# A dilated convolution on one core: warm-up matmuls taken out, the first load split in two, the last two stores split into four

## The chip, the cores and the metric

The kernel runs on one core of a Trainium2 chip. The metric is the device time of an execution, in microseconds (us). Each kernel of a comparison is run several times, in rounds that alternate it with the kernel before on the same chip. The profile is one execution, traced; its span is about 1.8 us shorter than the time of that execution.

In the text and in the views, PE is the matrix engine (TensorE) and PEld its weight loads; DVE is VectorE, ACT ScalarE, POOL or Pool GpSimd, SP SyncE. PEclk, the granted clock, is the share of PE's full clock that it was given. DMA means the transfers between HBM and SBUF. A semaphore is a counter on which an engine waits until others have raised it. Dummy matmuls are matmuls whose results nobody uses.

## The reference

```python
# x: [16, 64, 64, 64] float32, weight: [128, 64, 3, 3] float32, dilation 2
x_pad = np.pad(x, ((0, 0), (0, 0), (2, 2), (2, 2)))
for b, co, ci, kh, kw in all_of_them:
    output[b, co] += weight[co, ci, kh, kw] * x_pad[b, ci, kh*2:kh*2+h, kw*2:kw*2+w]
```

The output is [16, 128, 64, 64] float32. So 17.07 MB must be read from HBM and 33.55 MB written, whatever the arithmetic looks like. Stores are two thirds of the traffic.

## The kernel before

Two images of 64 channels fill the 128 partitions: an image pair. There are eight pairs, 0 to 7, and a pair is computed in four groups of 16 rows. A group needs 30 matmuls into three PSUM tiles; ScalarE copies one of them to SBUF, and VectorE adds it to each of the other two, into the output tile `osb`. The parts that matter here, shortened:

```python
XB = 4                                    # four float32 image pairs fit in SBUF
x32pool = tc.tile_pool(name="x32pool", bufs=XB)
opool   = tc.tile_pool(name="opool", bufs=3)      # three output tiles, 4 MB each

def load(pb, rows):                       # rows: where to cut, [H] is one transfer
    ...
    for hi in rows:
        nc.sync.dma_start(out=t[:, lo * W : hi * W], in_=x_pair[pb, :, lo * W : hi * W])

def store(pb, m, lo, hi):                 # Pool issues, but SP for the last pair
    queue = nc.gpsimd if pb < npairs - 1 else nc.sync
    queue.dma_start(out=out_img[2 * pb + m, :, lo * W : hi * W], in_=o_tiles[pb][...])

nc.sync.dma_start(out=w32, in_=weight...)         # weights first
for pb in range(min(XB, npairs)):
    load(pb, [H])
...
run_warm(14)                              # 14 dummy matmuls of 512 columns on zeros
# ... weights cast, transposed on PE, copied to w_sb ...
run_warm(14)                              # 14 more, until the first image is there
...
for G in range(ngroups):                  # 32 groups
    ...                                   # 30 matmuls, p_sb copy, two adds, casts ahead
    if ahead[0] >= NG * (freed[0] + 1) and freed[0] + XB < npairs:
        load(freed[0] + XB, [H])          # when all of an old pair is cast
    if pb in (0, npairs - 1) and g % 2 == 1:      # first and last pair: in halves
        for m in range(2):
            store(pb, m, (g - 1) * GR, (g + 1) * GR)
    elif 0 < pb < npairs - 1 and g == NG - 1:     # others: whole images
        for m in range(2):
            store(pb, m, 0, H)
```

A whole image is stored in rows of 16 KB per partition, half an image in rows of 8 KB, a quarter in rows of 4 KB. They show up in the trace as packets of those sizes.

Of the kernel before, what the change touches and what calls it, by code (L numbers as in the profile page):

```python
# [10 lines left out]
def kernel(  # L11
# [18 lines left out]
    nc = tc.nc  # L30

    B, CI, H, W = x.shape
# [5 lines left out]
    d = 2  # L38

    P = 128  # L40
    f32 = mybir.dt.float32
    f16 = mybir.dt.float16
# [4 lines left out]
    GR = 16  # L47
    NG = H // GR
    NBLK = GR // 4
    NH = GR // 2 * W  # L50
    npairs = B // 2
# [5 lines left out]
    wpool = ctx.enter_context(tc.tile_pool(name="wpool", bufs=1))  # L57
# [4 lines left out]
    ppool = ctx.enter_context(tc.tile_pool(name="ppool", bufs=1, space=bass.MemoryType.PSUM))  # L62
# [10 lines left out]
    def load(pb, rows):  # L73

        t = x32pool.tile([P, HW], f32, tag="x32", name="x32")
        x32_tiles[pb] = t
        lo = 0
        for hi in rows:
            nc.sync.dma_start(out=t[:, lo * W : hi * W], in_=x_pair[pb, :, lo * W : hi * W])
            lo = hi  # L80
# [19 lines left out]
    def store(pb, m, lo, hi):  # L100
        queue = nc.gpsimd if pb < npairs - 1 else nc.sync
        queue.dma_start(  # L102
            out=out_img[2 * pb + m, :, lo * W : hi * W],
            in_=o_tiles[pb][:, m * HW + lo * W : m * HW + hi * W],
        )
# [4 lines left out]
    w32 = wpool.tile([CO, CI * KH * KW], f32, name="w32")  # L110
    nc.sync.dma_start(out=w32, in_=weight.rearrange("o i h w -> o (i h w)"))  # L111
    for pb in range(min(XB, npairs)):
        load(pb, [H])

    ident = wpool.tile([P, P], f16, name="ident")
    make_identity(nc, ident)


    warm = wpool.tile([P, 512], f16, name="warm")
    nc.vector.memset(warm, 0.0)  # L120
    wp = ppool.tile([P, 1024], f32, tag="p", name="wp")

    def run_warm(n):
        for _ in range(n):
            nc.tensor.matmul(out=wp[:, 0:512], lhsT=warm[:, 0:P], rhs=warm)  # L125

    run_warm(14)


    KINDS = 5  # L130
# [13 lines left out]
    for q, n in ((0, 8), (8, 7)):  # L144
        wt = apool.tile([P, 1024], f32, tag="ab", name="wt")
        for t in range(q, q + n):
            nc.tensor.matmul(
                out=wt[:, (t - q) * CO : (t - q + 1) * CO],
                lhsT=wd[:, t * 2 * CI : (t + 1) * 2 * CI],
                rhs=ident,  # L150
# [5 lines left out]
    def product(ps, src, kind, blk0, nblk, first, last):  # L156

        for j in (1, 0, 2):
            dw = (j - 1) * d
            o0, o1 = max(0, -dw), W - max(0, dw)  # L160
            t = kind * KW + j
            for hb in range(2):
                pp = slice(hb * CI, (hb + 1) * CI)
                rhs = src(pp, dw + o0, dw + o1)
                po = ps[:, hb * NH + blk0 * 2 * W : hb * NH + (blk0 + nblk) * 2 * W]
                po = po.rearrange("p (r w) -> p r w", w=W)[:, :, o0:o1]
                nc.tensor.matmul(  # L167
                    out=po,
                    lhsT=w_sb[pp, t * CO : (t + 1) * CO],
                    rhs=rhs,  # L170
                    start=first and j == 1,
                    stop=last and j == 2,
                )

    def blocks(x16, b0, n, e):

        v = x16.rearrange("p (b e r w) -> p b e r w", e=2, r=2, w=W)
        return lambda pp, c0, c1: v[pp, b0 : b0 + n, e, :, c0:c1]

    run_warm(14)  # L180
    ahead = [0, 0]

    def prepare(casts, sums):

        while ahead[0] < min(casts, ngroups):
            cast(ahead[0])
            ahead[0] += 1
        while ahead[1] < min(sums, ngroups):
            rowsum(ahead[1])
            ahead[1] += 1  # L190
# [5 lines left out]
    for G in range(ngroups):  # L196
        pb, g = divmod(G, NG)
        x16 = x16_tiles[pb]
        xs = xs_tiles[pb].rearrange("p (r w) -> p r w", w=W)
        if g == 0:  # L200
            o_tiles[pb] = opool.tile([P, 2 * HW], f32, tag="osb", name="osb")
        o = o_tiles[pb].rearrange("p (m b e q) -> p m b e q", m=2, e=2, q=2 * W)
        b0 = g * NBLK

        psP = ppool.tile([P, 2 * NH], f32, tag="p", name="psP")
        sv = lambda pp, c0, c1: xs[pp, g * GR // 2 : (g + 1) * GR // 2, c0:c1]
        product(psP, sv, 0, 0, NBLK, True, True)

        psA = apool.tile([P, 2 * NH], f32, tag="ab", name="psA")
        product(psA, blocks(x16, b0, NBLK, 1), 1, 0, NBLK, True, False)  # L210
        z = 1 if g == 0 else 0
        product(psA, blocks(x16, b0 + z - 1, NBLK - z, 1), 2, z, NBLK - z, False, True)

        psB = apool.tile([P, 2 * NH], f32, tag="ab", name="psB")
        product(psB, blocks(x16, b0, NBLK, 0), 3, 0, NBLK, True, False)
        z = 1 if g == NG - 1 else 0
        product(psB, blocks(x16, b0 + 1, NBLK - z, 0), 4, 0, NBLK - z, False, True)

        p_sb = spool.tile([P, 2 * NH], f32, tag="psb", name="p_sb")
        nc.scalar.copy(out=p_sb, in_=psP)  # L220
        pv = p_sb.rearrange("p (m b q) -> p m b q", m=2, q=2 * W)

        def evac(e, ps):
            nc.vector.tensor_tensor(  # L224
                out=o[:, :, b0 : b0 + NBLK, e],
                in0=ps.rearrange("p (m b q) -> p m b q", m=2, q=2 * W),
                in1=pv,
                op=add,
            )

        evac(0, psA)
        prepare(min(G + 3 + (G + 1) // 2, G + 1 + LOOK), G + 3)
        evac(1, psB)

        if ahead[0] >= NG * (freed[0] + 1) and freed[0] + XB < npairs:
            load(freed[0] + XB, [H])
            freed[0] += 1
        if pb in (0, npairs - 1) and g % 2 == 1:
            for m in range(2):
                store(pb, m, (g - 1) * GR, (g + 1) * GR)  # L240
        elif 0 < pb < npairs - 1 and g == NG - 1:
            for m in range(2):
                store(pb, m, 0, H)
# [35 lines left out]
```

## Time and profile before

| | before |
|---|---|
| time, median of 3 (lowest to highest) | 127.46 us (127.44 to 127.64) |
| span of the profiled execution | 125.6 us |
| moved by DMA | 50.78 MB, mean 404 GB/s |
| last VectorE add ends | 111.9 us |
| last data packet ends | 124.0 us |
| last store's semaphore full | 124.5 us |

From the profile page of the kernel before: busy time by engine, then rows of the span in 40 slices of 3.14 us, each digit a busy share in tenths; GB/s is what DMA moved in each slice.

```profile
PE 108.3 (86%) x1003; PEld 53.8 (43%) x1003; DVE 89.9 (72%) x105; ACT 66.9 (53%) x71; POOL 9.3 (7%) x22
...
PE   6998999999999999999979999999999999920000
...
DMA  5999999999999999999999999999999999999970
GB/s 160 383 444 418 438 423 402 381 415 444 391 457 418 410 418 436 441 444 418 423 423 425 428 449 423 428 418 423 428 449 423 428 428 418 412 431 407 428 331 16
```

Two rows are full of nines, PE and DMA, and the reader must find out which of them the time follows. PE stops at slice 36; DMA goes on for three slices after it.

The chain of work that ended last, kernel before, in order of time (start us, length us, what), with the stretch from 67.2 to 108.1 us, all PE, left out:

```profile
37.37 0.52 POOL out_dram L102
37.89 26.48 DMA out_dram<-osb
64.37 0.03 issue
...
64.49 1.24 DVE osb L224
65.73 0.04 issue
65.77 1.44 PE psB L167 x12
...
108.13 1.28 PE psA L167 x12
```

VectorE waited until 64.4 us for a store of pair 1 to leave an output tile free, and PE waited for VectorE. After that PE runs back to back to its end.

The start of the kernel before, from the timeline (start us, busy us, engine, line, operation, out<-in, shapes, count, and the idle time just before with what ended it):

```profile
1.19 5.08 PE L125 MATMUL wp<-warm 128*128 128x512 f16 x14 [1.19 <-DVE warm L120]
...
6.11 1.00 PE L147 MATMUL wt<-ident,wd 128*128 128x128 f16 x15
...
6.95 3.19 PE L125 MATMUL wp<-warm 128*128 128x512 f16 x14
...
8.80 2.10 ACT L88 CAST x_157<-x_80 128x1152 f16<-128x1152 f32 x2 [0.25 <-DMA x_80<-in_x_dram]
...
10.47 0.81 PE L167 MATMUL psP<-xs,w_sb 64*128 64x512 f16 x6 [0.34 <-DVE xs L98]
```

The dummies fill PE from 1.2 us until the first image pair is loaded and cast. The granted clock becomes full at 5.05 us.

The table by stretch, kernel before (stretch in us, its length, busy time and count of PE, weight loads, VectorE, ScalarE and Pool, granted clock, DMA share, GB/s). A DMA share of 1.00 means that all 16 DMA engines had a packet in progress.

```profile
core 0: us, PE busy (x) PEld busy (x) DVE busy (x) ACT busy (x) POOL busy (x), PEclk, DMA share, GB/s
...
20.00:25.00 5.00, 5.00 (x52) 2.43 (x50) 4.35 (x7) 4.06 (x5) 0.00 (x0) 1.00 1.02 388
25.00:32.00 7.00, 7.00 (x69) 3.21 (x66) 6.04 (x7) 4.71 (x5) 1.05 (x2) 1.00 0.99 414
...
99.00:107.00 8.00, 8.00 (x80) 4.37 (x78) 6.88 (x8) 2.89 (x3) 1.06 (x2) 1.00 1.00 422
107.00:120.00 13.00, 3.51 (x36) 1.70 (x31) 4.11 (x4) 1.01 (x1) 0.00 (x0) 0.78 1.00 420
```

### The profile page before, as it was taken

Reading aid. Unit: us, or ns where it says so; the run is one execution under the profiler, and the core shown is the slowest. Engines: PE = TensorE matmul, PEld = TensorE weight load, DVE = VectorE, ACT = ScalarE, POOL = GpSimd, SP = SyncE. Lnnn points to the kernel's source line nnn. Section 1 sums busy time; section 2 is a strip of 40 time slices with the busy share of each in tenths; the row PEclk is TensorE's granted clock in tenths of the full one; section 3 lists DMA queues with packets and bytes.
Section 4 is the critical chain, followed back from the end, with each engine's and each line's share of the span. In section 5 each row is a group of like instructions: output and inputs, shape, how many; then the busy total and the mean of one; then the engine's idle time right before and its main releaser. Section 6 shows DMA issues by size and latency. Waiting matters only on the chain.

```text
span 125.6 us, 2342 instructions
## 1 busy us (share of the span) xinstructions
PE 108.3 (86%) x1003; PEld 53.8 (43%) x1003; DVE 89.9 (72%) x105; ACT 66.9 (53%) x71; POOL 9.3 (7%) x22
## 2 busy tenths in 40 slices
PE   6998999999999999999979999999999999920000
PEld 2453444544454445444435555555555555500000
DVE  0732888988898888988649998889888988760000
ACT  4558686966666666666654666666666433300000
POOL 2000003030002001100210003000200120000000
PEclk9999999999999999999999999999999999997555
DMA  5999999999999999999999999999999999999970
GB/s 160 383 444 418 438 423 402 381 415 444 391 457 418 410 418 436 441 444 418 423 423 425 428 449 423 428 418 423 428 449 423 428 428 418 412 431 407 428 331 16
DMA packets 4186, 50.78 MB, mean 404 GB/s; under 512 B 464, under 2 KB 464, under 8 KB 592
## 3 DMA queue, kind: packets, MB, share of 16 engines
q0 software_dynamic: 2304, 29.36, 55.1%
q1 hardware_dynamic: 1872, 21.27, 40.8%
q8 instruction: 8, 0.13, 0.4%
q14 instruction: 2, 0.02, 0.0%
HBM read 17.07 MB, written 33.55 MB: 403 GB/s over the span
## 4 chain that ended last, share of the span: by engine, by line
PE 54%; DMA 27%; DVE 4%; DVEq 1%; ACT 1%; issue 1%; POOL 0%; SPq 0%
PE psA L167 22%; DMA out_dram<-osb 21%; PE psB L167 21%; PE psP L167 11%; DMA x_80<-in_x_dram 6%; DVE osb L224 4%; ACT x_157 L88 1%; DVEq L274 1%; DVE xs L98 1%; POOL out_dram L102 0%; SPq L111 0%; DVEq L224 0%
## 5 line engine op out<-in xcount | busy, mean ns | idle before, releaser
L167 PEld LDWEIGHTS <-w_sb 64*128 64x128 f16 x960 | 49.9, 94 | 50.6 <-issue 1.0
L220 ACT COPY p_sb<-psP 128x1024 f32<-128x1024 f32 x32 | 32.4, 1012 | 37.7 <-PE psP L167 18.2
L224 DVE TENSOR_TENSOR osb<-psA,p_sb 128x1024 f32<-128x1024 f32 x32 | 39.2, 1224 | 15.2 <-PE psA L167 11.7
L224 DVE TENSOR_TENSOR osb<-psB,p_sb 128x1024 f32<-128x1024 f32 x32 | 39.0, 1218 | 0.0
L167 PE MATMUL psP<-xs,w_sb 64*128 64x496 f16 (+1 forms) x192 | 25.7, 371 | 0.3 <-DVE xs L98 0.3
L102 POOL DMA_DIRECT2D out_dram<-osb x16 | 8.6, 540 | 91.3 <-DVE osb L224 91.3
L125 PE MATMUL wp<-warm 128*128 128x512 f16 x28 | 8.3, 460 | 1.2 <-DVE warm L120 1.2
L167 PE MATMUL psB<-x_695,w_sb 64*128 64x496 f16 (+3 forms) x48 | 5.6, 365 | 0.7 <-DVE osb L224 0.7
L167 PE MATMUL psB<-x_1017,w_sb 64*128 64x496 f16 (+3 forms) x48 | 5.6, 365 | 0.0
L167 PE MATMUL psB<-x_856,w_sb 64*128 64x496 f16 (+3 forms) x48 | 5.6, 365 | 0.0
L167 PE MATMUL psB<-x_1178,w_sb 64*128 64x496 f16 (+3 forms) x48 | 5.6, 365 | 0.0
L167 PE MATMUL psA<-x_1178,w_sb 64*128 64x496 f16 (+3 forms) x48 | 5.6, 365 | 0.0
L167 PE MATMUL psA<-x_1017,w_sb 64*128 64x496 f16 (+3 forms) x48 | 5.6, 365 | 0.0
L167 PE MATMUL psA<-x_856,w_sb 64*128 64x496 f16 (+3 forms) x48 | 5.6, 365 | 0.0
L167 PE MATMUL psA<-x_695,w_sb 64*128 64x496 f16 (+3 forms) x48 | 5.6, 365 | 0.0
L167 PE MATMUL psA<-x_157,w_sb 64*128 64x496 f16 (+3 forms) x48 | 5.6, 365 | 0.0
L167 PE MATMUL psA<-x_240,w_sb 64*128 64x496 f16 (+3 forms) x48 | 5.6, 365 | 0.0
L167 PE MATMUL psA<-x_532,w_sb 64*128 64x496 f16 (+3 forms) x48 | 5.6, 365 | 0.0
L167 PE MATMUL psA<-x_369,w_sb 64*128 64x496 f16 (+3 forms) x48 | 5.6, 365 | 0.0
L167 PE MATMUL psB<-x_240,w_sb 64*128 64x496 f16 (+3 forms) x48 | 5.6, 365 | 0.0
L167 PE MATMUL psB<-x_157,w_sb 64*128 64x496 f16 (+3 forms) x48 | 5.6, 365 | 0.0
L167 PE MATMUL psB<-x_369,w_sb 64*128 64x496 f16 (+3 forms) x48 | 5.6, 365 | 0.0
(35 smaller groups left out, 66.3 us busy)
## 6 DMA issues: line engine op xcount, KB each, us to landing
out_dram<-osb POOLq DMA_DIRECT2D x12, 2048.0 KB, 17.6
out_dram<-osb POOLq DMA_DIRECT2D x4, 1024.0 KB, 20.8
out_dram<-osb SPq DMA_DIRECT2D x4, 1024.0 KB, 11.8
x_80<-in_x_dram SPq DMA_DIRECT2D x1, 2048.0 KB, 7.6
x_82<-in_x_dram SPq DMA_DIRECT2D x1, 2048.0 KB, 12.0
x_84<-in_x_dram SPq DMA_DIRECT2D x1, 2048.0 KB, 17.9
x_86<-in_x_dram SPq DMA_DIRECT2D x1, 2048.0 KB, 23.8
x_245<-in_x_dram SPq DMA_DIRECT2D x1, 2048.0 KB, 17.5
```

The costliest lines, as they stand in the source:

```text
L88: nc.scalar.copy(out=x16_tiles[pb][:, lo * W : hi * W], in_=x32_tiles[pb][:, lo * W : hi * W])
L98: nc.vector.tensor_tensor(out=s, in0=v[:, :, 0], in1=v[:, :, 1], op=add)
L102: queue.dma_start(out=out_img[2 * pb + m, :, lo * W : hi * W], in_=o_tiles[pb][:, m * HW + lo * W : m * HW + hi * W],)
L125: nc.tensor.matmul(out=wp[:, 0:512], lhsT=warm[:, 0:P], rhs=warm)
L167: nc.tensor.matmul(out=po, lhsT=w_sb[pp, t * CO : (t + 1) * CO], rhs=rhs, start=first and j == 1, stop=last and j == 2,)
L220: nc.scalar.copy(out=p_sb, in_=psP)
L224: nc.vector.tensor_tensor(out=o[:, :, b0 : b0 + NBLK, e], in0=ps.rearrange("p (m b q) -> p m b q", m=2, q=2 * W), in1=pv, op=add,)
L274: with _tile.TileContext(nc) as tc:
```

## The change

The intent: drop the dummy matmuls; let the first half of pair 0 arrive early, so that work can start without waiting for all of it; store the last half images in quarters, so that SP issues 16 transfers in place of 13 and the very last one owns the last of the eight semaphores that are waited for at the end.

```diff
     for pb in range(min(XB, npairs)):
-        load(pb, [H])
+        load(pb, [H] if pb else [32 + d, H])
 ...
-    warm = wpool.tile([P, 512], f16, name="warm")
-    nc.vector.memset(warm, 0.0)
-    wp = ppool.tile([P, 1024], f32, tag="p", name="wp")
-
-    def run_warm(n):
-        for _ in range(n):
-            nc.tensor.matmul(out=wp[:, 0:512], lhsT=warm[:, 0:P], rhs=warm)
-
-    run_warm(14)
 ...
-    run_warm(14)
 ...
-        if pb in (0, npairs - 1) and g % 2 == 1:
+        if pb == npairs - 1 and g == NG - 1:
+            for m in range(2):
+                for lo in (2 * GR, 3 * GR):
+                    store(pb, m, lo, lo + GR)
+        elif pb in (0, npairs - 1) and g % 2 == 1:
             for m in range(2):
                 store(pb, m, (g - 1) * GR, (g + 1) * GR)
```

## The prediction

> **What bounds the kernel.** Transfers. The page's DMA row reads 9 tenths in slices 2 to 38 of 40; the table by stage gives a DMA share of 1.00 to 1.01 from 10.5 to 110.7 us at 416 to 429 GB/s. 50.6 MB cross HBM, 118 us at 429 GB/s. PE looks critical as well (the chain of waits gives it 54%, back to back from 65.8 to 109.4 us), but the last VectorE add ends at 111.9 us, while the DMA engines drain queued stores until 124.0 us (their packets). The last store's semaphore fills at 124.5 us; then come 1.1 us of closing waits, of which three pairs after that of the last store take 0.06 us each. So PE has microseconds to spare at the end. The chain also shows VectorE waiting for a store until 64.4 us: DMA set the pace.
>
> **Removed.** 28 dummy matmuls (8.3 us of PE, none on the DMA path). In the trace the matmul spacing falls at 5.0 us from 0.43 us, half of full speed: without the first 14 the transposes and first real groups will run at half clock. The Trainium skill (TensorE: Matmul & The Clock Gate, Part 1) says that full clock comes after about 3.4 us of sustained activity; this trace agrees roughly, 1.2 to 5.0 us. A full-speed group of 30 products takes 3.17 us; I estimate 2 to 4 us of PE work slowed by half, a loss of 1.5 to 3 us. The transposes, which waited for dummies until 5.9 us, can start about 1 us earlier, but at half speed. PE's end: hardly later, at most 3 us, because at the 64 us wait it meets DMA again: all loads are in by then, and the bytes moved fix when that store lands.
>
> **Added.** The first half of image pair 0 lands at about 6 us in place of 8.8. The first cast cannot use all of it: ScalarE copies weights until 8.6 us. The first product comes near 9.9 in place of 10.47. No bytes change. Packets: 8 KB took 309 ns, 16 KB 611 ns, hence about 7 ns per packet beyond its bytes. 2 MB of stores in 4 KB rows in place of 8 KB are 16 more packets per engine, +0.11 us; the split load +0.06 us (estimates).
>
> **Moved.** SP issues 16 transfers, not 13: with eight rotating semaphores the last store gets the last one waited for, saving three waits, 0.19 us, after the end. PE has 56 fewer instructions; the instruction queue moved eight 16 KB packets, the last at 111.5 us after PE's program had ended. It may vanish: up to 0.6 us, only if it sits on the slowest DMA engine.
>
> **Sum, on the critical path:** -0.19 (waits), +0.17 (packets), -0.2 (instruction packet, weighted by chance): about 0.2 to 0.3 us less. Split load and missing dummies should be worth nothing: DMA is saturated from 4 us on. Predicted 127.2 us, range 126.4 to 127.8 (8 in 10). Faster by over 2%: 3%; within 2%: 94%; slower by over 2%: 3%.
>
> **What would show it.** DMA row still 9s to slice 38; last data packets near 123.5 to 124.2 us; the closing wait on the last store followed at once by the drain; first psP product near 10 us, its group taking about 5 us; granted clock full only after 12 to 16 us; last VectorE add between 110 and 114 us.
>
> **What would make it wrong.** A clock that stays at half for long, so that PE ends after about 118 us; DMA queues running empty near 20 us because casts, and with them the release of load buffers, come late; 4 KB rows costing much more than 7 ns a packet; the spread between DMA engines at the end changing by a microsecond.

## The result, and the profile after

| | before | after |
|---|---|---|
| time, median of 6, same chip | 127.45 us (127.29 to 127.72) | 127.38 us (127.24 to 127.64) |
| ratio after to before | | 0.9995, 95% interval 0.9977 to 1.0012 |
| span of the profiled execution | 125.6 us | 125.8 us |
| first product starts | 10.47 us | 9.57 us |
| full granted clock from | 5.05 us | 14.29 us |
| stores of pair 6 issued from | 100.1 us | 100.6 us |
| last VectorE add ends | 111.9 us | 112.4 us |
| last data packet ends | 124.0 us | 124.5 us |

A ratio here is the mean time of one kernel's fast runs over that of the other's in the same rounds, so it is not quite the ratio of the medians in the table. The two kernels take the same time.

From the profile page after, the lines that answer to those of before:

```profile
PE 103.6 (82%) x975; PEld 53.6 (43%) x975; DVE 89.9 (71%) x104; ACT 66.9 (53%) x71; POOL 9.3 (7%) x22
...
PE   0519999999999999999999999999999999920000
...
DMA  4999999999999999999999999999999999999980
GB/s 130 374 439 448 427 427 417 383 414 453 414 411 432 443 414 448 427 419 422 438 432 427 435 417 422 432 437 432 417 427 427 437 391 427 422 393 430 405 327 18
```

PE now rests in the first slices, and the DMA row has not moved. Look at the slice that begins at 100.6 us, the 33rd: 391 GB/s, where before had 428. It is the first hint of what the prediction overlooked.

The start after, from the timeline:

```profile
4.34 0.50 PE L136 MATMUL wt<-ident,wd 128*128 128x128 f16 x3 [4.34 <-DVE wd L124]
...
5.16 1.64 PE L136 MATMUL wt<-ident,wd 128*128 128x128 f16 x12 [0.31 <-DVE wd L127]
...
7.91 2.10 ACT L88 CAST x_127<-x_80 128x1152 f16<-128x1152 f32 x2
...
9.57 1.44 PE L156 MATMUL psP<-xs,w_sb 64*128 64x512 f16 x6 [2.78 <-DVE xs L98]
...
14.90 0.81 PE L156 MATMUL psP<-xs,w_sb 64*128 64x512 f16 x6
```

The first half of the load had landed at 6.8 us, but the cast starts only near 8 us and without idle time ahead of it: ScalarE was copying weights until then. The first product starts 0.9 us earlier than before, as a result of the split load and of transposes that no longer queue behind dummies. The first group then takes 5.3 us (9.57 to 14.90) where a group at full clock takes 3.2: PE reaches the second group at 14.9 us, 1.4 us later than before (13.5). Such starts scatter, though: in the traces of four other kernels here that open exactly as the kernel before, the second group began between 13.7 and 14.6 us, later when the first load landed later.

The table by stretch, after:

```profile
20.00:25.00 5.00, 5.00 (x52) 2.66 (x50) 4.27 (x6) 3.71 (x4) 1.20 (x2) 1.00 1.01 398
25.00:32.00 7.00, 7.00 (x72) 3.62 (x68) 6.35 (x7) 4.69 (x5) 1.05 (x2) 1.00 0.99 422
...
99.00:107.00 8.00, 8.00 (x81) 4.10 (x78) 6.88 (x9) 3.04 (x3) 1.05 (x2) 1.00 0.99 412
107.00:120.00 13.00, 4.02 (x40) 1.92 (x36) 4.62 (x4) 1.01 (x1) 0.00 (x0) 0.74 0.99 413
```

From 99 to 107 us DMA moved 10 GB/s less than before. The page's share of 1.00 and 0.99 hides it; counting packets in half-microsecond steps shows the 16 DMA engines 87% and 78% busy in the two steps from 101.0 us (before 97% and 99%).

One more reading of the trace is needed. A transfer of 128 partitions raises its semaphore 16 times (29 transfers before, 464 arrivals), which is read here as once for each of the 16 DMA engines. The 16 times of the last store show how evenly the engines end:

| last store's 16 arrivals | first | median | 15th | last | from the last to the end of the span |
|---|---|---|---|---|---|
| before | 121.4 | 122.5 | 123.3 | 124.5 us | 1.08 us |
| after | 122.1 | 122.3 | 123.6 | 124.9 us | 0.90 us |

The end is set by one late engine in both kernels. The closing stretch is 0.18 us shorter after, as the intent said; the late engine is 0.45 us later in this one profiled execution, although the median engine is not.

### The profile page after: what moved, and what is told of

Same layout as the page of the kernel before. It is cut to its first block, busy times and chain, and to the rows that moved or that the text cites. A ratio compares the mean times of both kernels' runs of the same rounds, so it can differ in the third digit from the quotient of the medians.

```text
span 125.8 us, 2288 instructions
## 1 busy us (share of the span) xinstructions
PE 103.6 (82%) x975; PEld 53.6 (43%) x975; DVE 89.9 (71%) x104; ACT 66.9 (53%) x71; POOL 9.3 (7%) x22
## 4 chain that ended last, share of the span: by engine, by line
PE 81%; DVE 3%; DMA 2%; ACT 1%; DVEq 1%; issue 0%
PE psA L156 32%; PE psB L156 31%; PE psP L156 17%; DMA w_78<-in_weight_dram 2%; PE wt L136 1%; DVE osb L212 1%; DVEq L266 1%; ACT x_127 L88 1%; DVE wd L127 1%; DVE wd L124 1%; ACT w_sb L143 0%; DVE w_sb L142 0%; DVE xs L98 0%; DVEq L212 0%
## 5 line engine op out<-in xcount | busy, mean ns | idle before, releaser
L156 PEld LDWEIGHTS <-w_sb 64*128 64x128 f16 x960 | 52.3, 95 | 51.8 <-issue 5.1
L156 PE MATMUL psP<-xs,w_sb 64*128 64x496 f16 (+1 forms) x192 | 26.5, 379 | 2.8 <-DVE xs L98 2.8
L156 PE MATMUL psA<-x_127,w_sb 64*128 64x496 f16 (+3 forms) x48 | 6.7, 420 | 0.0
L156 PE MATMUL psB<-x_127,w_sb 64*128 64x496 f16 (+3 forms) x48 | 6.3, 397 | 0.0
L136 PE MATMUL wt<-ident,wd 128*128 128x128 f16 x15 | 2.1, 309 | 4.7 <-DVE wd L124 4.3
L156 PE MATMUL psB<-x_502,w_sb 64*128 64x496 f16 (+3 forms) x48 | 5.6, 365 | 0.0
L156 PE MATMUL psB<-x_210,w_sb 64*128 64x496 f16 (+3 forms) x48 | 5.6, 365 | 0.0
L156 PE MATMUL psB<-x_339,w_sb 64*128 64x496 f16 (+3 forms) x48 | 5.6, 365 | 0.0
L156 PE MATMUL psB<-x_665,w_sb 64*128 64x496 f16 (+3 forms) x48 | 5.6, 365 | 0.0
L156 PE MATMUL psB<-x_826,w_sb 64*128 64x496 f16 (+3 forms) x48 | 5.6, 365 | 0.0
L156 PE MATMUL psB<-x_987,w_sb 64*128 64x496 f16 (+3 forms) x48 | 5.6, 365 | 0.0
L156 PE MATMUL psB<-x_1148,w_sb 64*128 64x496 f16 (+3 forms) x48 | 5.6, 365 | 0.0
L156 PE MATMUL psA<-x_339,w_sb 64*128 64x496 f16 (+3 forms) x48 | 5.6, 365 | 0.0
L156 PE MATMUL psA<-x_502,w_sb 64*128 64x496 f16 (+3 forms) x48 | 5.6, 365 | 0.0
L156 PE MATMUL psA<-x_987,w_sb 64*128 64x496 f16 (+3 forms) x48 | 5.6, 365 | 0.0
L156 PE MATMUL psA<-x_210,w_sb 64*128 64x496 f16 (+3 forms) x48 | 5.6, 365 | 0.0
L156 PE MATMUL psA<-x_665,w_sb 64*128 64x496 f16 (+3 forms) x48 | 5.6, 365 | 0.0
L156 PE MATMUL psA<-x_826,w_sb 64*128 64x496 f16 (+3 forms) x48 | 5.6, 365 | 0.0
## 6 DMA issues: line engine op xcount, KB each, us to landing
x_298<-in_x_dram SPq DMA_DIRECT2D x1, 2048.0 KB, 14.9
```

The lines of the kernel that those rows point to most:

```text
L136: nc.tensor.matmul(out=wt[:, (t - q) * CO : (t - q + 1) * CO], lhsT=wd[:, t * 2 * CI : (t + 1) * 2 * CI], rhs=ident,)
L156: nc.tensor.matmul(out=po, lhsT=w_sb[pp, t * CO : (t + 1) * CO], rhs=rhs, start=first and j == 1, stop=last and j == 2,)
```

## The experiments

Twelve kernels ran, all with correct results, in three calls. "Before" is the kernel before on the same chip in the same rounds: medians 127.50, 127.44 and 127.42 us of 11 runs. The scatter should be kept in mind: single runs of the kernel before went up to 128.26 us.

### The parts of the change, one by one

**No dummies, nothing else.** The kernel before without the definition of `run_warm` and its two calls.

```diff
-    warm = ...; wp = ...; def run_warm(n): ...
-    run_warm(14)
 ...
-    run_warm(14)
```

> The kernel before without its 28 dummy matmuls, nothing else. Theory (DMA engines are saturated, PE has slack): ratio to before 0.998 to 1.002; full clock only near 14 us, as in the changed kernel; last VectorE add 0 to 2 us later than 111.9 us; last data packet still 123.5 to 124.5 us. Rival (PE paces the kernel, and in the changed kernel a loss of about 1.4 us there was paid back by the split load): +0.8 us or more, ratio 1.006 or more.

Measured: 127.70 us, ratio 1.0033, interval 1.0000 to 1.0066. The full clock came at 15.9 us, the last VectorE add ended at 113.8 us, the stores of pair 6 were issued at 102.0 us. The table by stretch has DMA short near 101 us:

```profile
99.00:107.00 8.00, 8.00 (x82) 4.35 (x80) 7.32 (x9) 2.68 (x4) 1.05 (x2) 1.00 0.93 389
```

Neither wording fits well. The time rose by less than the rival asked for, and the interval ends just at 1. One run of six, at 129.11 us, makes up about half of the rise of the mean. But DMA lost 33 GB/s over 8 us, about 0.6 us of its full rate, in a place where the prediction had seen only saturation.

**Split load, nothing else.**

```diff
-        load(pb, [H])
+        load(pb, [H] if pb else [32 + d, H])
```

> The kernel before with only the first load split in two. Theory: PE may start earlier, but the transfers behind it land about 0.15 to 0.2 us later (in the changed kernel the second transfer of 2 MB landed at 13.5 us, before at 13.4), so +0.1 to +0.2 us, ratio 1.000 to 1.002. Rival (an earlier first product is worth something): -0.4 us or more, ratio 0.997 or less.

Measured: 127.52 us, ratio 1.0003, interval 0.9989 to 1.0016: no difference that can be told. The median arrival of the next load was at 13.60 us, before 13.36.

**Quarters, nothing else.** The `if` and `elif` of the change, in the kernel before.

> The kernel before with only the last half images in quarters. SP then issues 15 transfers, so the last store has the last semaphore but one. Theory: two of three closing waits saved (-0.12 us), packets of 4 KB instead of 8 KB +0.1 us: ratio 0.998 to 1.002, and the trace shows about 0.95 us from the last landing to the end in place of 1.1. Rival (smaller last transfers let the end start sooner, or balance the DMA engines): -0.5 us or more, ratio 0.996 or less.

Measured: 127.38 us, ratio 0.9989, interval 0.9977 to 1.0001. From the last arrival to the end 0.95 us, as expected. The rival fails.

**No dummies and the split load, without quarters.** The two edits above together.

> Without dummies and with the split first load, without quarters: the missing cell between the run that only drops the dummies (ratio 1.0033, 95% interval 1.0000 to 1.0066) and the one that only splits the load (1.0003). If the split load pays back what the missing dummies cost (PE 2.8 us behind the kernel before at the second group without it, 1.4 us behind with it), ratio 0.999 to 1.001 and store issues of image pair 6 near 100.6 us. If the load does nothing for it, ratio 1.002 to 1.006, store issues near 102 us.

Measured: 127.78 us, ratio 1.0025, interval 0.9990 to 1.0060: inconclusive in time. The six times fall in two sets, 127.42 to 127.47 and 128.10 to 128.54. In the trace the split load did pay back PE's loss: pair 6 was stored from 100.6 us and not 102.0 (one trace of each kernel, and such starts scatter by about 1 us).

**The whole change with the dummies put back.** `run_warm` and its calls are restored in the changed kernel.

> The changed kernel with its dummies put back. 16 transfers of SP, so the last store has the last semaphore, and PE as early as in the kernel before. If removing the dummies is free in the presence of the split load: ratio 0.998 to 1.001, the same as the changed kernel. If the dummies are still worth something: 0.995 to 0.998.

Measured: 128.06 us, ratio 1.0035, interval 0.9994 to 1.0077; again two sets, 127.45 to 127.69 and 128.43 to 128.82. Neither expectation is met, and this kernel is not shown to improve on either.

The kernel before has such slower runs too (128.05 and 128.26 of its 11). The profiled executions of these two kernels both fell in the slower set, and the arrivals show what sets them apart from the kernel before:

| last store's arrivals | time of that run | median engine | 15th | last engine |
|---|---|---|---|---|
| before | 127.34 us | 122.5 | 123.3 | 124.5 us |
| no dummies, split load | 128.10 us | 122.3 | 123.6 | 125.3 us |
| change with dummies | 128.50 us | 122.5 | 124.2 | 125.8 us |

The median engine ends at the same time; the last engine alone is 0.8 to 1.3 us later. So what these two slower executions lost is, in their traces, the lateness of one DMA engine; no trace of a faster execution of the same kernels was kept to compare. Why it differs from execution to execution stays open.

**The closing waits** can be read from these traces without a stopwatch. SP had issued 13, 14, 15 or 16 transfers in these kernels, and the stretch from the last arrival to the end was 1.08 (before, 13), 1.01 (both kernels with only the load split, 14), 0.95 (quarters, 15) and 0.90 us (16, with and without dummies): 0.06 us for each wait saved, as predicted.

### How late may PE be?

**PE about 4 us late.** In the changed kernel, 34 dummies just before the first real matmuls.

```diff
+    # warm, wp and run_warm as in the kernel before
 ...
+    run_warm(34)
     ahead = [0, 0]
```

> The changed kernel with 34 dummy matmuls just before the first real ones, which should put PE about 4 us behind the changed kernel all the way (last VectorE add near 116 us). Theory 1 (as predicted: PE has 7 us of slack at the end, since the last DMA engine drains until 124 us): +0 to +0.5 us, ratio 1.000 to 1.004. Theory 2 (the slack is small and lies near 101 us, where the stores of image pair 5 run out before those of pair 6 are issued; the changed kernel's faster DMA engines idle there already, and only the late engine's 2 us or so of lag hide it): the DMA row shows a hole near 103 to 106 us and the time rises by 1.2 to 2.5 us, ratio 1.009 to 1.02. Rival (PE paces everything): +4 us, ratio 1.031.

Measured: 130.69 us, ratio 1.0233, interval 1.0196 to 1.0271. The last VectorE add ended at 116.8 us, 4.4 us later than after. From the profile page of this run:

```profile
DMA  5999999898999999999999999999999949999991
GB/s 148 360 446 416 451 431 411 304 315 340 441 424 416 444 424 439 426 426 439 416 426 426 439 416 431 431 431 421 391 416 446 411 198 406 421 424 403 413 407 47
```

and from its table by stretch:

```profile
20.00:25.00 5.00, 5.00 (x50) 2.70 (x48) 4.04 (x5) 4.50 (x5) 0.48 (x1) 1.00 0.89 347
25.00:32.00 7.00, 7.00 (x73) 3.96 (x70) 6.35 (x8) 5.21 (x6) 1.77 (x4) 1.00 0.97 330
...
99.00:107.00 8.00, 8.00 (x83) 4.47 (x79) 7.37 (x9) 3.62 (x5) 1.05 (x2) 1.00 0.81 336
```

Seven microseconds of slack at the end do not exist. DMA loses time at two places. Near 103 to 106 us the stores of pair 5 are nearly done and pair 6 is not (198 GB/s in the 33rd slice); its stores are issued at 105.07 us and their first packets start at 106.17. Counting packets in progress, the engines idled 1.69 us on average from 99 to 107 us (before 0.02): this is a hole. The other place was named in the prediction as what could make it wrong, but not in this run's expectation: near 22 to 32 us. ScalarE, which copies `psP` for every group, casts the image pairs in between, so a late PE makes late casts. The load of pair 4 was issued at 22.1 us (before 16.2, after 17.6), when the four pairs loaded before it were nearly all in and the first store was not yet issued (24.5).

Only part of this early loss is a queue that ran empty: the engines idled 0.65 us on average from 20 to 32 us (before 0.04). From 26 to 30 us they were busy all the time, as the share of 0.97 in the table hints, and still moved only 221 to 384 GB/s, because load packets of 16 KB took 0.75 to 1.10 us on average in place of 0.61. Why they did was not found.

The two losses add up. DMA moved in the three stretches 8,214 KB before (5 x 388 + 7 x 414 + 8 x 422) and 6,733 KB here. The missing 1,481 KB are 3.45 us at 429 GB/s: 1.85 us in the first two stretches, 1.60 us in the last. The measured difference of medians is 3.25 us; the two traced executions differ by 3.63 us. The sum is not exact: from 32 to 99 and from 107 to 120 us another 251 KB, 0.6 us, are missing.

**The same, and every pair stored in halves.**

```diff
-        elif pb in (0, npairs - 1) and g % 2 == 1:
+        elif g % 2 == 1:
```

> The same late PE (34 dummy matmuls), with every image pair stored in halves as soon as a half is done, so that the stores do not run out while a whole pair is computed. Theory 2: the hole near 104 us goes and the time returns to that of the kernel before, ratio 0.998 to 1.004. If the time of the run with the late PE came from anything but stores running out (PE itself, load buffers released late), it stays as slow as that run.

Measured: 130.44 us, ratio 1.0229, interval 1.0201 to 1.0257. The hole near 104 us is gone (every half-microsecond step from 29 to 123 us is over 95% busy), but the time did not return. Taken alone, this would have felled the theory. The next run shows part of the reason.

**Kernel before, every pair stored in halves.**

```diff
-        if pb in (0, npairs - 1) and g % 2 == 1:
+        if g % 2 == 1:
```

> The kernel before with every image pair stored in halves. Theory 2 with its second part (the end is set by the latest DMA engine, which does not idle near 101 us in the kernel before): the idle of the other engines near 101 us (about 0.4 us) goes, but the time stays, ratio 0.998 to 1.002. Rival (that idle is time lost): ratio 0.997 or less.

Measured: 128.25 us, ratio 1.0063, interval 1.0048 to 1.0078. Both wordings miss: halves cost 0.8 us. The trace has 1,536 more data packets, 96 for each engine. A packet of 16 KB took 611 ns and one of 8 KB 309 ns, so two halves take 7 ns more than a whole; 96 times 7 ns is 0.67 us, most of it. So in the run ahead of this one about 0.8 us of packets had been laid over what closing the hole gave back. Even then 3.25 - 1.60 + 0.8 gives +2.45 us, and +3.0 was measured; 0.55 us of that run stays unexplained. (The execution that was traced was the fastest of its four, 2.53 us above the traced one of the kernel before.) The kernel before also had hardly a hole to fill: from 99 to 107 us its engines idled 0.02 us by the count of packets in progress, not the 0.4 us that the expectation names.

**Late PE, pair 6 alone in halves.** This closes the hole near 104 us with a sixth as many extra packets.

```diff
-        elif pb in (0, npairs - 1) and g % 2 == 1:
+        elif pb in (0, npairs - 2, npairs - 1) and g % 2 == 1:
```

> The run with 34 dummies and PE about 4 us late (ratio 1.0233), with image pair 6 alone stored in halves, which costs only 128 more packets of 8 KB per image (estimate +0.1 us). If the hole near 104 us is what cost the time: the hole goes, ratio 1.006 to 1.014. If the cost lies in the first 30 us (load of image pair 4 issued at 22 us, when the loads before it land at 23 us: DMA rate of 158 to 375 GB/s from 22 to 25 us): ratio 1.018 to 1.024. Both places can share it: 1.014 to 1.018.

Measured: 129.72 us, ratio 1.0176, interval 1.0136 to 1.0216. Its table by stretch:

```profile
20.00:25.00 5.00, 5.00 (x52) 2.68 (x48) 4.05 (x5) 4.61 (x5) 0.59 (x1) 1.00 0.91 338
25.00:32.00 7.00, 7.00 (x72) 3.89 (x70) 6.36 (x8) 5.10 (x6) 1.66 (x4) 1.00 0.98 349
...
99.00:107.00 8.00, 8.00 (x82) 4.47 (x80) 7.37 (x9) 3.62 (x5) 1.72 (x4) 1.00 0.98 410
```

The late hole is closed (410 GB/s for 336), the early one is not (338 and 349 for 347 and 330). By the same sum 801 KB are missing, 1.87 us; measured +2.3 us. The traced executions differ by 1.96 us. So both places share the cost of a late PE, by the bytes. In time this is less firm: the ratio fell from 1.0233 to 1.0176 with intervals that overlap, on two chips, and no run closed the early place alone. This is the third of the three expectations, at the edge to the second.

**Kernel before, PE 2 us late.**

```diff
-    run_warm(14)          # the second call
+    run_warm(23)
```

> The kernel before with 9 more dummies before the first real matmuls, at full clock, so that PE starts about 2 us later and nothing else changes. At 64 to 66 us PE has about 0.9 us of waiting for a store to give up, so the stores of image pair 6 should be issued about 1.1 us later than 100.1 us. Theory (little slack there, hidden partly by the lag of the latest engine): idle of the DMA engines near 101 to 103 us of about 1 us, and +0.1 to +0.6 us, ratio 1.001 to 1.005. As predicted at first (7 us of slack): ratio 0.999 to 1.001.

Measured: 127.54 us, ratio 1.0003, interval 0.9978 to 1.0028. Pair 6 was stored from 101.1 us, 1.0 us later than before: the other microsecond was given up at the 64 us wait, as expected. Counting packets in progress, the engines idled 0.4 us on average between 5 and 120 us (before 0.1), and the time did not rise. The late engine would explain how that can be: its share of the last store of pair 5 arrived at 104.7 us, 1.2 us after the next engine's, so it had packets while the others waited for pair 6. An idle moment of fifteen engines would then be free as long as the sixteenth is the one that ends last. The run without dummies agrees: its engines idled 0.8 us on average from 99 to 107 us, and its last store's median arrival came 0.9 us later than before (123.4 for 122.5 us), but the last arrival only 0.2 us later (124.7 for 124.5 us).

### What the late engine is not

**Kernel before, all stores issued by SP.** Theory A is that the late engine and the long packets both come from the transfers that Pool issues.

```diff
-        queue = nc.gpsimd if pb < npairs - 1 else nc.sync
+        queue = nc.sync
```

> The kernel before with all stores issued by SP instead of Pool for all but the last image pair. What is left at the end in both kernels is one DMA engine that finishes about 1.2 us after the next and 2 to 3 us after most, and near 21 to 24 us the packets of loads become longer (up to 1 us in place of 0.61) just as the first stores issued by Pool begin. Theory A[...]: the long packets near 21 us go, the engines finish within 1 us of each other, and the time falls by 1 to 2.5 us (ratio 0.98 to 0.992). Theory B (the late engine is late for another reason, such as the instruction packets): the same 1 us or more of lateness and ratio 0.996 to 1.01. Loads now queue behind stores in one queue; if that starves PE, the time rises by several us.

Measured: 127.82 us, ratio 1.0029, interval 1.0014 to 1.0044. Theory A falls as an explanation of the end: the last store's arrivals spread from 121.2 to 124.9 us. The slow stretch of loads did not go either, it moved (304 GB/s in the slice from 25.2 us, when SP's queue came to the first stores). One part of A seems to survive: in the kernel before, the last engine fell behind the 15th from 0.06 us at 64.4 us to 1.6 us at 109.7 us, while only Pool's stores ran; with SP's stores that gap shrank, from 1.3 to 0.3 us, over the same stretch. But it shrank with Pool's stores as well: in the trace of the next run, which is the kernel before up to its last store, from 1.33 us at 65.6 us to 0.12 us at 99.6 us. So this gap does not tell the two apart. The Trainium skill (DMA: Bandwidth & Descriptors, Latency and other measured facts) says that two of the 16 engines are usually slower, and gives as a best guess the descriptor rings of transfers issued from GpSimd. No run here shows it: the lateness remains without such transfers, and the records name no engine.

**Less work for one engine.** The idea rests on an assumption that no record shows: that the engine numbered highest serves partitions 120 to 127. A last store that leaves them out would take its eight packets of 8 KB from it (2.4 us at 309 ns each).

```diff
+        parts = ((120, 128), (0, 120)) if (pb, m, hi) == (npairs - 1, 1, H) else ((0, P),)
+        for p0, p1 in parts:
             queue.dma_start(out=out_img[2 * pb + m, p0:p1, ...], in_=o_tiles[pb][p0:p1, ...])
```

> The kernel before with the very last store of 1 MB issued as partitions 120 to 127 and then 0 to 119[...]. If the engine that ends 1.2 us after the next one is that one: last landing about 123.3 to 123.7 us in place of 124.5, ratio 0.993 to 0.997. If it is another: last landing 124.5 to 124.9 us, ratio 1.000 to 1.004. In both cases one engine should be done about 2.4 us earlier than it was.

Measured: 127.70 us, ratio 1.0019, interval 1.0005 to 1.0034. The last store has 15 arrivals in place of 16, so one engine was left out, but this tells nothing about the late one: the transfer of 120 partitions itself ran slowly. From 120 to 124 us DMA moved 224 to 333 GB/s, packets of 8 KB took up to 2.2 us, and its arrivals came between 123.0 and 125.2 us. Which engine is late stays open.

## Why the prediction was right

**The time: right.** 127.2 us was predicted and 127.38 measured, in the range, and "within 2%" was right. The predicted gain of 0.2 to 0.3 us is no larger than what the interval leaves open (0.3 us less to 0.15 us more), so the runs confirm that nothing changed, and not the sum of terms.

**DMA bounds the kernel: right.** Bytes, the DMA row and the median engine's end (122.5 and 122.3 us) did not change.

**Missing dummies and split load are worth nothing: right for the whole, for a thinner reason than given.** "DMA is saturated from 4 us on" was read from averages. In truth the DMA queue runs out at two places when PE is late: near 23 us, if the load of pair 4 comes late (0.65 us idle with 34 dummies, and slow packets after it), and near 101 us, where the last stores of pair 5 end just as those of pair 6 are issued (1.69 us idle). The changed kernel is 1.4 us late at the second group, gives 0.9 us back because it no longer has to wait at 64 us (there is no DMA wait there in its chain), and reaches pair 6 half a microsecond late. That is free, as the run with 2 us shows. The prediction had foreseen the wait at 64 us but not looked at the hand-over near 101 us; that the loss fitted in there was luck.

**The step that failed: "So PE has microseconds to spare at the end."** The spare time was measured at the wrong place, at the last store, where 12 us of queued stores hide anything. It has to be measured at each hand-over, where one batch of transfers runs out and the next has to be there. Ending the last add 1.0 us later than the kernel before was free within 0.3%; ending it 4.9 us later cost 3.25 us, although it ended at 116.8 us, before the 118 us that the prediction named as the limit.

**The sum of small terms: the signs right, nearly all unresolved in time.** The waits gave 0.18 us (predicted 0.19), read in the trace. For 16 packets more per engine 0.11 us was estimated; the run with 96 more cost 0.8 us, so a sixth of it, 0.13 us, agrees, and so do the packets themselves (4 KB took 159 ns, two of them 9 ns more than one of 8 KB, 0.14 us for 16). The split load was estimated at 0.06 us; the second load arrived about 0.15 us later (its median arrival was at 13.57 us on average in the seven traces with a split load, at 13.42 us in the seven without), so this term looks too small, although the time of the run with it alone rose by nothing that can be told. The eighth packet of the instruction queue did vanish (7 in place of 8), and the predicted mean gain of 0.2 us from it did not show: the late engine was not earlier. These terms cancel to within the scatter.

**What would show it.** First product "near 10 us" was 9.57, its group 5.3 us for "about 5", full clock 14.29 us within "12 to 16", last add 112.4 us within "110 and 114". The last data packet, at 124.49 us, missed "123.5 to 124.2": the late engine.

**Not settled:** whether dropping the dummies alone costs 0.3%, since that interval ends at 1.0000; which engine is late, and why by more in some executions; why loads slow down just before the first stores, which made up most of the early loss of the late PE. No kernel tried here is clearly faster than the kernel before or the changed one; the nearest is quarters alone, at 0.9989 with an interval that includes 1.

## What to carry to other kernels

When transfers bound a kernel, look for slack where the queue of transfers comes closest to running empty, at the hand-over between batches, and not where the last compute ends. A row of nines does not show such a place; delaying the compute by a known amount does. Read GB/s beside the busy share, since busy engines can move less: here 330 GB/s at a share of 0.97. Before cutting transfers finer to remove a hole, count the packets: here every extra one of 8 KB cost about 7 ns on its engine, and 96 for each engine cost the kernel before 0.8 us, where there was hardly a hole to fill.

## What the Trainium skill lacked or had wrong

- TensorE: Matmul & The Clock Gate, Part 1, puts full clock about 4 us into sustained matmuls, give or take 500 ns, and says that the moment depends on a free-running window. In the eight kernels here that start with dummies at 1.2 us it came 2.8 to 5.9 us after the first of them (at 4.03 to 7.07 us; before 3.9 us after), and 4.7, 5.2 and 3.5 us after the first real product in three kernels without dummies, which had run 15 transposes 5 us earlier. This is a wider spread than those 500 ns, though the same part also says that the number of slow matmuls of one kernel varies from run to run.
- DMA: Bandwidth & Descriptors, Specifications, gives about 1 us to the first byte of a transfer issued from GpSimd. With the engines nearly idle this agrees: 1.1 us (105.07 to 106.17 us, late PE; 31% and 21% busy in the two half-microseconds from 105.0 us). While loads ran, the first store took 4.3 us from issue to its first packet (18.68 to 22.95 us, before) and 4.9 us with the late PE (24.52 to 29.47 us); the page has no such figure.
- The same page, Latency and other measured facts, explains late engines, as its best guess, by transfers from GpSimd alone. Without any such transfer the last engine still ended 2.5 us after the median one (124.9 and 122.4 us).
- The same page, Why small descriptors are slow, has a fixed overhead per packet in cycles and calls packing worthwhile only for very small ones. No page has what it adds up to at large sizes: 309 ns for 8 KB, 611 ns for 16 KB, and 0.8 us for a kernel that stores its inner pairs in 8 KB rows in place of 16 KB.
- No page has the cost of the semaphore waits that close a kernel: 0.06 us for each pair here.
- No page says that loads slow down when the first stores start: packets of 16 KB took up to 1.06 us in place of 0.61 between 20.5 and 23 us (before), and 0.75 to 1.10 us on average from 26 to 30 us with the late PE, both with stores from Pool issued and their first packet still to come; the slow stretch came also with stores from SP.
